# Inverse block products as 32x32 products on the array's diagonal, tied products in the mixers' steps, and x's squares summed on GpSimd, in a one-layer RWKV-7 and gated-delta-rule trunk

## The chip, the cores and the metric

The kernel runs on one core of one Trainium2 chip. The time is the device time of one execution in microseconds (us). Before the change it is 1283.71 us, the median of three runs (1283.25 to 1285.89).

## What is computed

One layer works on x, 256 tokens by 2048 features, all in float32:

```
h = rms_norm(x);  proj = h @ w_in                      # 2048 x 6448
y_a = rwkv7_mixer(proj[:, :3360])                      # 16 heads of 64
y_b = gdn_mixer(proj[:, 3360:])                        # 8 value heads of 128, 4 key heads
x = x + concat(y_a, y_b) @ w_out                       # 2048 x 2048
h = rms_norm(x)
x = x + (silu(h @ w_gate) * (h @ w_up)) @ w_down       # 2048 x 5632, twice, and 5632 x 2048
out = rms_norm(x)
```

Each mixer is a recurrence over time. Both are computed in four chunks of 64 tokens. Inside a chunk the recurrence is a triangular system, so each mixer needs the inverse of a unit triangular 64x64 matrix for each head and chunk, and then passes a state from chunk to chunk. rms_norm needs, for each token, the sum of x's squares over the features.

## The kernel before, in words

**Projections.** Weights come as blocks of 128x1024 (`raw`, three buffers, loaded by SyncE's queue, L168). `halves_of` cuts each block in two halves and splits each half in a high part on ScalarE (`wh`, L177) and a low part on VectorE (`wl`, L178), with four buffers of each. A block of w_in or w_out then gives 24 TensorE products of 256 columns (L199 to L201: high by high, high by low, low by high), of w_gate and w_up 16 (L196, L197), of w_down 24 (L1060). PSUM tag `pb` holds two outputs of projections.

**The mixers run beside the projections.** `prep` (RWKV, per half of the heads), `chain` (RWKV's chunk steps), `gdn_v` and `gdn` are generators, stepped by `tick()` after each group of products. The framework then sets the order of every engine's instructions by a simulated timeline with priorities: what is ready first there stands first. On the chip each engine takes its instructions in that order and waits where an operand is missing.

**Inverses.** `tri_inverse` is called three times: `r` for each RWKV half, `g` for the gated delta rule. It solves 32x32 triangles by a substitution on VectorE (`X`, L325 and L327, 31 steps), writes the result to memory (`sX`, L333) and reads it back in another layout (`st`, L336). The missing off-diagonal 32x32 block of each 64x64 inverse is a product of three 32x32 blocks: first F = B by the one diagonal inverse (`psF`, L351), then F by the other (`psO`, L362). There are 32 such blocks. Four of them are laid on the diagonal of a 128x128 tile that is zero elsewhere (`Bd` and `Fd`, cleared by GpSimd at L338 and L344), so that one product of 128 by 128 by 32 does four blocks: 8 products for `psF`, 8 for `psO`. `Bd` takes the buffer of the substitution's input `A` (tag `i1`), so it is cleared and loaded (`load_bd`, L525 or L837) when the substitution has ended. `tn` (L346, VectorE) is the transposed first half of `st`.

**Steps of the mixers.** RWKV's chunk step has the products R (L545), U (L553), S (L564), Y from the state (L583) and Y from U and V (L585), each as 8 products for 4 pairs of heads and 2 heads, on 64 rows or 64 columns of the array. The delta rule's step has `psK` (L863, full array), `psUg` (L874, 8 products on 64x64), `psSg` (L888, 4 products on 64 rows) and `psOg` (L901, 8 on 64x64). `prep` has `ps_w` and `ps_a` (L403, L404), low-rank products on the upper and the lower 64 rows. A float32 product stands in the trace as two records, one of fp32r as one.

**x's squares.** For the first norm four groups of squares (`sqx`, ScalarE, L274) are halved by VectorE into `ssb` (L275), and 8 float32 products with a constant matrix sum them over partitions (L277), in front of `rstd` (L279, L280).

**The last unit's weights.** The final four feed-forward rows are kept split in SBUF (`wend`, places listed by `wend_slots`), in tiles that the mixers have left.

Of the kernel before, what the change touches and what calls it, by code (L numbers as in the profile page):

```python
# [17 lines left out]
P = 128  # L18
# [31 lines left out]
def trunk_kernel(ctx, tc, xT, vecs, fnw, w_up, a_up, g_up, w_in, w_ab, w_out, w_gu, w_dn, out):  # L50
# [220 lines left out]
    for q in range(4):  # L271
# [39 lines left out]
    def tri_inverse(ip, load_blocks, load_bd, store, dst, nm, psk, sign=1):  # L311
# [3 lines left out]
        load_blocks(A)  # L315
        X = ip.tile([P, 16, 32], F32, tag="i2", name=f"X_{nm}")
# [26 lines left out]
        Fd = ip.tile([P, 8, P], F32, tag="i2", name=f"Fd_{nm}")  # L343
        G.memset(Fd, 0.0)  # L344
# [5 lines left out]
        for g in range(8):  # L350
            PE.matmul(psF3[:, g, :], Bd[:, g, :], tn[:, g, :], start=True, stop=True)  # L351
        for q in range(4):
            qs = slice(q * 32, q * 32 + 32)
            if q % 2:
                S.activation(Fd[qs, :, qs], psF3[qs], AF.Copy, scale=float(sign))
            else:
                V.tensor_scalar(Fd[qs, :, qs], psF3[qs], float(sign), None, ALU.mult)
# [3 lines left out]
        for g in range(8):  # L361
            PE.matmul(psO3[:, g, :], Fd[:, g, :], st[:, 1, g, :], start=True, stop=True)  # L362
# [13 lines left out]
    def prep(hf):  # L376
# [15 lines left out]
        for gr in range(2):  # L392
# [3 lines left out]
            th, sq, al = [], [], []  # L396
            k2 = kt[key]
            sq = rp.tile([P, 2, T], F32, tag="sq2", name=f"sq{hf}{gr}")
            for pi in range(2):
                p = gr * 2 + pi  # L400
                f = hf * 4 + p
                ts = slice(pi * T, pi * T + T)
                PE.matmul(psw[:, ts], lw[0:64, p * P:p * P + P], twa[0:64, :], start=True, stop=True)  # L403
                PE.matmul(psa[:, ts], lw[64:128, p * P:p * P + P], twa[64:128, :], start=True, stop=True)  # L404
                S.activation(sq[:, pi, :], k2[:, pi, :], AF.Square, scale=vc("k_k", f))
            for pi in range(2):
# [97 lines left out]
    def chain(hf):  # L504
# [34 lines left out]
        for ch in range(NCH):  # L539
# [10 lines left out]
            for p in range(4):  # L550
                for h in range(2):
                    hr = slice(h * 64, h * 64 + 64)
                    PE.matmul(U3[hr, p, :], ar[hr, p, ch, 0, :], RR[hr, p, :], start=True, stop=True)  # L553
            for h in range(2):
                hr = slice(h * 64, h * 64 + 64)
                (S.copy, V.tensor_copy)[h](UV[0:64, ch, :, hr], U3[hr])
            yield None
            if ch < NCH - 1:
                psS = mps("psS", "mc")
                S3 = psS[:, 0:256].rearrange("p (a v) -> p a v", a=4)  # L560
                for p in range(4):
                    for h in range(2):
                        hr = slice(h * 64, h * 64 + 64)
                        PE.matmul(S3[hr, p, :], bkn[:, p, ch, hr], UV[:, ch, p, hr], start=True, stop=True)  # L564
# [15 lines left out]
            ph = [(p, h, slice(h * 64, h * 64 + 64)) for p in range(4) for h in range(2)]  # L580
            if ch:
                for p, h, hr in ph:
                    PE.matmul(Y3[hr, p, :], ar[hr, p, ch, 1, :], St[hr, p, :], start=(p == 0), stop=False)  # L583
            for p, h, hr in ph:
                PE.matmul(Y3[hr, p, :], AT[:, h, p, ch, 64:128], UV[:, ch, p, hr], start=(ch == 0 and p == 0),  # L585
                           stop=(p == 3))
# [138 lines left out]
    def gdn():  # L725
# [467 lines left out]
```

## Time and profile before

| | |
|---|---|
| median of the runs | 1283.71 us (1283.25 to 1285.89) |
| the profiled execution's own time | 1289.42 us |
| its span, first to last instruction | 1287.7 us |
| instructions | 23086 |
| TensorE busy (matrix products) | 1264.9 us, 98% |
| weight loads into TensorE | 1127.3 us, 88% |
| VectorE | 930.3 us, 72% |
| ScalarE | 726.7 us, 56% |
| GpSimd | 18.1 us, 1% |
| mean granted TensorE clock | 0.994 of 2.4 GHz |

The projections through w_in and the mixers beside them fill the first 430 us or so, w_out follows to about 540 us, and the feed-forward takes the rest. Busy times of matrix products overlap, since they are pipelined; what a product costs is read from the distance between the starts of neighbours.

### The profile page before, as it was taken

What the parts mean: (1) busy time and instruction counts of PE and PEld (TensorE: products, weight loads), DVE (VectorE), ACT (ScalarE), POOL (GpSimd) and SP (SyncE); (2) the same over time, 40 slices, a digit from 0 to 9 for tenths busy, and PEclk for the clock granted to TensorE, in tenths of its full rate; (3) what the DMA queues carried; (4) which work ended last, traced back from release to release, by engine and by line L of the source; (5) the groups of instructions that cost most, each with busy time, mean ns of one, the idle gap of its engine ahead of it and who ended that gap; (6) DMA issues with size and microseconds to landing.
All of it is one profiled execution on the core that took longest, in us unless ns stands there. A gap on an engine that the chain in (4) does not pass through costs nothing.

```text
span 1287.7 us, 23086 instructions
## 1 busy us (share of the span) xinstructions
PE 1264.9 (98%) x8458; PEld 1127.3 (88%) x8458; DVE 930.3 (72%) x1981; ACT 726.7 (56%) x1469; POOL 18.1 (1%) x66
## 2 busy tenths in 40 slices
PE   8999999999999999999999999999999999999997
PEld 7999999999998899988888888888888888888886
DVE  6988796978864878767766766666767676767664
ACT  7675665666644656666655555545454545555552
POOL 1000000000000000000000000000000000000000
PEclk9999999999999999999999999999999999999999
DMA  7455556464564345556765555555555556565541
GB/s 241 147 167 173 148 171 150 153 183 125 147 211 148 107 141 196 181 171 222 247 195 182 194 184 192 183 194 188 189 188 189 191 186 193 182 196 186 190 148 65
DMA packets 108129, 226.80 MB, mean 176 GB/s; under 512 B 52272, under 2 KB 54448, under 8 KB 107760
## 3 DMA queue, kind: packets, MB, share of 16 engines
q1 hardware_dynamic: 103744, 222.19, 55.2%
q10 hardware_dynamic: 4128, 2.10, 0.6%
q8 instruction: 66, 1.08, 0.3%
q0 software_dynamic: 144, 1.05, 0.2%
q14 instruction: 47, 0.39, 0.1%
HBM read 218.75 MB, written 4.46 MB: 173 GB/s over the span
## 4 chain that ended last, share of the span: by engine, by line
PE 91%; DMA 4%; DVE 2%; ACT 1%; SPq 1%; issue 0%; DVEq 0%; ACTq 0%
PE psb L196 23%; PE psd L1060 17%; PE psb L197 12%; PE psb L201 10%; PE psb L200 9%; PE psb L199 9%; DMA raw_end<-in_w_dn 2%; PE ps_A L464 1%; DVE wl L178 1%; PE psd L1098 1%; PE psd L1096 1%; PE psd L1097 1%; PE psUg L874 1%; DMA raw<-in_w_gu 1%; PE psSg L888 0%; DVE wend L178 0%
## 5 line engine op out<-in xcount | busy, mean ns | idle before, releaser
L177 ACT ACTIVATE wh<-raw 128x512 fp32r<-128x512 f32 x780 | 488.3, 630 | 424.6 <-PE psb L196 137.6
L178 DVE TENSOR_TENSOR wl<-raw,wh 128x512 fp32r<-128x512 f32 x780 | 534.6, 689 | 264.3 <-ACT wh L177 261.1
L196 PE MATMUL psb<-x2s,wh 128*128 128x512 f32 x1408 | 497.4, 398 | 0.0
L197 PE MATMUL psb<-x2s,wl 128*128 128x256 f32 x1408 | 395.2, 282 | 1.5 <-DVE wl L178 1.5
L196 PEld LDWEIGHTS psb<-x2s,wh 128*128 128x128 f32 x1408 | 263.9, 188 | 63.4
L197 PEld LDWEIGHTS psb<-x2s,wl 128*128 128x128 f32 x1408 | 265.9, 189 | 4.9 <-DVE wl L178 2.8
L199 PE MATMUL psb<-xs,wh 128*128 128x256 f32 x816 | 237.1, 291 | 6.3 <-ACT wh L177 6.3
L201 PE MATMUL psb<-xs,wl 128*128 128x256 f32 x816 | 237.1, 292 | 1.7 <-DVE wl L178 1.7
L200 PE MATMUL psb<-xs,wh 128*128 128x256 f32 x816 | 236.9, 291 | 0.0
L1060 PE MATMUL psd<-wh,h 128*128 128x512 f32 x640 | 199.2, 389 | 0.0
L199 PEld LDWEIGHTS psb<-xs,wh 128*128 128x128 f32 x816 | 158.8, 195 | 9.0 <-ACT wh L177 6.3
L201 PEld LDWEIGHTS psb<-xs,wl 128*128 128x128 f32 x816 | 158.6, 195 | 5.0 <-DVE wl L178 3.4
L200 PEld LDWEIGHTS psb<-xs,wh 128*128 128x128 f32 x816 | 158.7, 195 | 3.7 <-issue 2.5
L1060 PEld LDWEIGHTS psd<-wh,h 128*128 128x128 f32 x640 | 119.4, 188 | 24.9
L1060 PE MATMUL psd<-wl,h 128*128 128x512 f32 x320 | 124.4, 389 | 0.0
L200 PE MATMUL psb<-ys,wh 128*128 128x256 f32 x256 | 73.3, 287 | 1.3 <-DVE ys L223 1.3
L199 PE MATMUL psb<-ys,wh 128*128 128x256 f32 x256 | 73.5, 289 | 0.3 <-ACT ys L222 0.3
L201 PE MATMUL psb<-ys,wl 128*128 128x256 f32 x256 | 73.0, 285 | 0.0
L1060 PEld LDWEIGHTS psd<-wl,h 128*128 128x128 f32 x320 | 60.1, 188 | 12.6
L1066 DVE TENSOR_TENSOR acc<-acc,psd 128x512 f32<-128x512 f32 x80 | 51.2, 681 | 2.5 <-PE psd L1060 2.5
L200 PEld LDWEIGHTS psb<-ys,wh 128*128 128x128 f32 x256 | 49.0, 191 | 2.8 <-DVE ys L223 1.7
L199 PEld LDWEIGHTS psb<-ys,wh 128*128 128x128 f32 x256 | 48.8, 191 | 1.8 <-issue 1.2
(316 smaller groups left out, 1088.5 us busy)
## 6 DMA issues: line engine op xcount, KB each, us to landing
raw<-in_w_gu SPq DMA_DIRECT2D x176, 512.0 KB, 3.6
raw<-in_w_in SPq DMA_DIRECT2D x99, 512.0 KB, 3.6
raw<-in_w_dn SPq DMA_DIRECT2D x80, 512.0 KB, 3.5
raw<-in_w_out SPq DMA_DIRECT2D x32, 512.0 KB, 3.5
raw_end<-in_w_dn SPq DMA_DIRECT2D x8, 512.0 KB, 3.9
xraw<-in_xT SPq DMA_DIRECT2D x8, 256.0 KB, 5.8
x<-in_xT SPq DMA_DIRECT2D x1, 2048.0 KB, 11.2
raw<-in_w_ab SPq DMA_DIRECT2D x2, 512.0 KB, 6.0
```

The costliest lines, as they stand in the source:

```text
L177: S.activation(wh, raw[:, hs], AF.Copy)
L178: V.tensor_tensor(wl, raw[:, hs], wh, ALU.subtract)
L196: PE.matmul(ps, wh[:, ks], rt[:, ri, :], start=st, stop=False)
L197: PE.matmul(ps[:, T:], wl[:, ks], rt[:, ri, 0:T], start=False, stop=sp)
L199: PE.matmul(ps[:, 0:T], wh[:, ks], rt[:, ri, 0:T], start=st, stop=False)
L200: PE.matmul(ps[:, 0:T], wh[:, ks], rt[:, ri, T:], start=False, stop=False)
L201: PE.matmul(ps[:, 0:T], wl[:, ks], rt[:, ri, 0:T], start=False, stop=sp)
L464: PE.matmul(psA[h][:, ch, :], bk[hr, ch].rearrange("p a t -> p (a t)"), ar[hr, p, ch].rearrange("p a t -> p (a t)"), start=True, stop=True)
L874: PE.matmul(u3[h % 2 * 64:h % 2 * 64 + 64, h // 2, :], TT[rows, 2 * h + cp, :], vn[rows, cp, h, :], start=True, stop=True)
L1060: PE.matmul(banks[tb * 2 + cg], st, parts[cg][w], start=(i == 0 and w == 0 and st is hh), stop=(i == n - 1 and st is hl))
L1066: V.tensor_tensor(acc[:, tb, cs], acc[:, tb, cs], banks[tb * 2 + cg], ALU.add)
L1096: PE.matmul(ps, hh, wh, start=(i == 0), stop=False)
```

## The change

Four things change.

- **Inverses.** The zero-filled 128x128 tiles go. `Bd` and `Fd` hold 32 columns, get tags of their own (`i5`, `i6`), and `Bd` is loaded at the start of the inverse. `psF` and `psO` become 32 products each of 32 by 32 by 32, at the four diagonal places of the array. One VectorE operation copies `psF` to `Fd` where two of VectorE and two of ScalarE did.
- **Tied products.** `together(ms, after)` makes each product of a list depend, in order alone, on the one ahead of it, and lets the first wait for all operations in `after`. Tied are: the four `ps_w` and `ps_a` products of a group (`low`); the eight of RWKV's U; RWKV's S and both Y products of a chunk, after both copies of U (`my`, `uv`); the four `psK`, after the eight updates of the state (`mk`, `news`); the eight `psUg`, after the eight updates of `vn` (`ready`); and `psSg` with `psOg`, after both copies of `psUg` (`mo`, `ready`).
- **x's squares.** GpSimd adds the four `ssb` groups into one, and 2 products sum it instead of 8.
- **Places.** The tiles of `wend` are listed anew, with one `act` tile in place of `i2` and two fewer of its own.

```diff
+    def together(ms, after=(), sync=True):
+        kind = mybir.DependencyClass
+        for a in after:
+            tc.add_manual_dep(ms[0].ins, a.ins.name, mybir.DependencyInfo(kind.Sync, mybir.DependencyReason.DATA),
+                              reason="together")
+        for a, b in zip(ms, ms[1:]):
+            tc.add_manual_dep(b.ins, a.ins.name, mybir.DependencyInfo(kind.NoSync, mybir.DependencyReason.DATA),
+                              reason="together")
...
         V.tensor_tensor(ssb[:, q], sqx[:, 0:2, :], sqx[:, 2:4, :], ALU.add)
-        for m in range(2):
-            PE.matmul(ps[:, 0:T], half.to_broadcast([P, P]), ssb[:, q, m, :], start=(q == 0 and m == 0),
-                       stop=(q == 3 and m == 1))
+        if q:
+            G.tensor_tensor(ssb[:, 0], ssb[:, 0], ssb[:, q], ALU.add)
+    together([PE.matmul(ps[:, 0:T], half.to_broadcast([P, P]), ssb[:, 0, m, :], start=(m == 0), stop=(m == 1))
+              for m in range(2)])
...
+        Bd = ip.tile([P, 8, 32], F32, tag="i5", name=f"Bd_{nm}")
+        load_bd(Bd)
...
-        Bd = ip.tile([P, 8, P], F32, tag="i1", name=f"Bd_{nm}")
-        G.memset(Bd, 0.0)
-        load_bd(Bd)
...
-        for g in range(8):
-            PE.matmul(psF3[:, g, :], Bd[:, g, :], tn[:, g, :], start=True, stop=True)
...
+        diag = [(g, slice(q * 32, q * 32 + 32)) for g in range(8) for q in range(4)]
+        for g, qs in diag:
+            PE.matmul(psF3[qs, g, :], Bd[qs, g, :], tn[qs, g, :], start=True, stop=True)
+        V.tensor_scalar(Fd, psF3, float(sign), None, ALU.mult)
...
-        for g in range(8):
-            PE.matmul(psO3[:, g, :], Fd[:, g, :], st[:, 1, g, :], start=True, stop=True)
+        for g, qs in diag:
+            PE.matmul(psO3[qs, g, :], Fd[qs, g, :], st[qs, 1, g, :], start=True, stop=True)
...
+            together(low)
...
+            together([PE.matmul(U3[hr, p, :], ar[hr, p, ch, 0, :], RR[hr, p, :], start=True, stop=True)
+                      for p, h, hr in ph])
...
+            together(my, uv)
...
+                together(mk, news)
...
+            together([PE.matmul(u3[h % 2 * 64:h % 2 * 64 + 64, h // 2, :], TT[rows, 2 * h + cp, :],
+                                vn[rows, cp, h, :], start=True, stop=True) for h in range(8)], ready)
...
+            together(mo, ready)
...
-            w = rp.tile([P, 2, 512], F32R, tag="i2", name="wend")
-            yield w[:, 0, :]
-            yield w[:, 1, :]
+            w = act.tile([P, 4, 2 * T], F32R, tag="act", name="wend")
+            for i in range(4):
+                yield w[:, i, :]
```

In the changed program a line of the kernel before has a number 10 to 15 higher: L199 to L201 are L209 to L211 there, L874 is L883, L168 is L178.

**TensorE, the second chunk's `psUg`** (`psUg` is U of the delta rule, `psb` a projection's output). Before:

```order
L874 MATMUL psUg<-vnknSg,TTg 64x128 x2
L199 MATMUL psb<-xs_145,wh 128x256
L874 MATMUL psUg<-vnknSg,TTg 64x128 x2
L200 MATMUL psb<-xs_145,wh 128x256
L201 MATMUL psb<-xs_145,wl 128x256
L874 MATMUL psUg<-vnknSg,TTg 64x128 x2
L199 MATMUL psb<-xs_145,wh 128x256
L874 MATMUL psUg<-vnknSg,TTg 64x128
L200 MATMUL psb<-xs_145,wh 128x256
L874 MATMUL psUg<-vnknSg,TTg 64x128
```

Now:

```order
L210 MATMUL psb<-xs_145,wh 128x256
L211 MATMUL psb<-xs_145,wl 128x256
L883 MATMUL psUg<-vnknSg,TTg 64x128 x8
L209 MATMUL psb<-xs_145,wh 128x256
L210 MATMUL psb<-xs_145,wh 128x256
```

Eight products that stood in five pieces stand in one. Over the whole program `psUg` stands in 15 pieces before and in 5 now.

**SyncE's queue, the inverse `g`** (`X_g` is the substitution's result, `sX_g` and `st_g` its way through memory, `Bd_g` the block B, `TTg` the inverse's place). Before:

```order
L333 DMA sX_g<-X_g 1024x1x32 x2
L837 DMA Bd_g<-sG 32x4x32 x3
L168 DMA raw<-in_w_in 128x1024
L336 DMA st_g<-sX_g 128x8x32 x2
L837 DMA Bd_g<-sG 32x4x32 x2
L168 DMA raw<-in_w_in 128x1024
L837 DMA Bd_g<-sG 32x4x32 x3
L842 DMA TTg<-sX_g 32x16x32 x2
```

Now:

```order
L834 DMA A_g<-sG 16x32x32 x3
L842 DMA Bd_g<-sG 32x4x32 x6
L178 DMA raw<-in_w_in 128x1024
L842 DMA Bd_g<-sG 32x4x32 x2
L178 DMA raw<-in_w_in 128x1024 x5
L610 DMA yl_3613<-in_g_up 128x512
L964 DMA x_6047<-in_xT 128x4096
L611 DMA yl_3613<-in_g_up 32x512
L178 DMA raw<-in_w_in 128x1024 x6
L1029 DMA raw_end<-in_w_dn 128x1024
L346 DMA sX_g<-X_g 1024x1x32 x2
L178 DMA raw<-in_w_in 128x1024
```

The eight loads of `Bd_g` stand ahead of the substitution, next to those of its input `A_g`, instead of behind its result.

**TensorE, the third chunk's S and Y of RWKV's first half.** Before:

```order
L200 MATMUL psb<-xs_244,wh 128x256
L564 MATMUL psS<-UV_485,bkn_484 64x64
L201 MATMUL psb<-xs_244,wl 128x256
```

and nine products of projections further

```order
L200 MATMUL psb<-xs_145,wh 128x256
L564 MATMUL psS<-UV_485,bkn_484 64x64 x7
L583 MATMUL psY<-St_1837,ar_482 64x64 x8
L585 MATMUL psY<-UV_485,AT_483 64x64 x8
L201 MATMUL psb<-xs_145,wl 128x256
```

Now these stand in one piece:

```order
L569 MATMUL psS<-UV_482,bkn_481 64x64 x8
L587 MATMUL psY<-St_1877,ar_479 64x64 x8
L589 MATMUL psY<-UV_482,AT_480 64x64 x8
```

The first product no longer stands alone.

## Rows read from the trace of the kernel before

**Rows 1.** The page's first part, busy time of TensorE (PE) and its weight loads (PEld), share of the span, instructions; and the page's chain of work that ended last, by engine.

```profile
PE 1264.9 (98%) x8458; PEld 1127.3 (88%) x8458; DVE 930.3 (72%) x1981; ACT 726.7 (56%) x1469; POOL 18.1 (1%) x66
...
PE 91%; DMA 4%; DVE 2%; ACT 1%; SPq 1%; issue 0%; DVEq 0%; ACTq 0%
```

**Rows 2.** The list of waits of PE: who waited for whom, us in total, times, longest.

```profile
PE psF_g L351 <- DMA Bd_g<-sG: 2.2, 1, 2.2
PE psb L201 <- DVE wl L178: 1.7, 3, 0.8
...
PE psF_r L351 <- DMA ar<-sX_r: 1.6, 1, 1.6
```

**Rows 3.** Busy time by stretch, for a stretch in the mixers: start:end, length, busy us and instructions of PE, PEld, DVE, ACT, POOL, then the granted clock, the DMA engines' share and GB/s.

```profile
208.00:300.00 92.00, 92.00 (x932) 86.13 (x930) 73.98 (x218) 58.23 (x158) 4.59 (x11) 1.00 0.57 152
```

**Rows 4.** Timeline of PE around the first sum of squares: start us, us, engine, line, operation, records.

```profile
21.32 1.02 PE L277 MATMUL ps_ss<-ssb,vec 128*128 128x256 f32 x4
...
22.30 0.28 PE L200 MATMUL psb<-xs,wh 128*128 128x256 f32 x1
```

**Rows 5.** Timeline of PE around `ps_w` and `ps_a`: one product of each, neighbours, and later two products of `ps_w` alone. One projection product lies in each of the gaps.

```profile
39.44 0.48 PE L403 MATMUL ps_w<-twa,lw 64*128 64x256 f32 x1
...
40.29 0.28 PE L199 MATMUL psb<-xs,wh 128*128 128x256 f32 x1
...
177.81 1.13 PE L403 MATMUL ps_w<-twa,lw 64*128 64x256 f32 x4
...
179.10 0.28 PE L200 MATMUL psb<-xs,wh 128*128 128x256 f32 x1
```

**Rows 6.** Timeline of PE around RWKV's U in one piece, and S in two pieces of 1 and 7 products. One projection product lies in the first gap and one in the second.

```profile
241.77 0.28 PE L201 MATMUL psb<-xs,wl 128*128 128x256 f32 x1
241.98 0.68 PE L553 MATMUL psU<-RR,ar 64*64 64x64 f32 x16
...
242.81 0.28 PE L200 MATMUL psb<-xs,wh 128*128 128x256 f32 x1
...
245.54 0.33 PE L564 MATMUL psS<-UV,bkn 128*64 128x64 f32 x2
...
246.02 0.28 PE L199 MATMUL psb<-xs,wh 128*128 128x256 f32 x1
...
247.06 0.68 PE L564 MATMUL psS<-UV,bkn 128*64 128x64 f32 x14
247.67 0.68 PE L583 MATMUL psY<-St,ar 64*64 64x64 f32 x16
```

**Rows 7.** Timeline of PE around the delta rule's second `psUg` (five pieces, six projection products in the gap), `psSg` and `psOg` (one piece each, one projection product in the gap).

```profile
414.95 0.44 PE L874 MATMUL psUg<-vnknSg,TTg 64*64 64x128 f32 x4
...
418.36 0.28 PE L199 MATMUL psb<-xs,wh 128*128 128x256 f32 x1
...
445.54 1.13 PE L888 MATMUL psSg<-gates,vnknSg 64*128 64x256 f32 x4
...
446.82 0.28 PE L200 MATMUL psb<-ys,wh 128*128 128x256 f32 x1
...
450.92 1.09 PE L901 MATMUL psOg<-vnknSg,gates 64*64 64x128 f32 x16
...
452.16 0.28 PE L200 MATMUL psb<-ys,wh 128*128 128x256 f32 x1
```

**Rows 8.** Timeline of PE around `psF` of the three inverses; in brackets the idle time before and what ended it.

```profile
200.80 0.28 PE L200 MATMUL psb<-xs,wh 128*128 128x256 f32 x1
202.68 2.15 PE L351 MATMUL psF_r<-tn_r,Bd_r 128*128 128x32 f32 x16 [1.60 <-DMA ar<-sX_r]
204.64 0.56 PE L201 MATMUL psb<-xs,wl 128*128 128x256 f32 x1
...
283.87 1.87 PE L351 MATMUL psF_r<-tn_r,Bd_r 128*128 128x32 f32 x16
285.57 0.36 PE L200 MATMUL psb<-xs,wh 128*128 128x256 f32 x1
...
382.47 0.28 PE L200 MATMUL psb<-xs,wh 128*128 128x256 f32 x1
384.97 3.40 PE L351 MATMUL psF_g<-tn_g,Bd_g 128*128 128x32 f32 x16 [2.22 <-DMA Bd_g<-sG]
388.18 0.56 PE L201 MATMUL psb<-xs,wl 128*128 128x256 f32 x1
```

**Rows 9.** Busy time by stretch (columns as in Rows 3) behind the two long waits.

```profile
204.20:207.80 3.60, 3.60 (x19) 3.60 (x19) 2.45 (x6) 1.52 (x3) 0.00 (x0) 0.53 0.57 224
...
388.10:392.10 4.00, 4.00 (x20) 4.00 (x20) 1.53 (x3) 1.38 (x3) 0.00 (x0) 0.51 0.86 264
```

**Rows 10.** Timeline of VectorE and SyncE's queue in the inverse `g`: the substitution's last step, the transposed half `tn_g`, and the last loads of `Bd_g`.

```profile
372.15 0.18 DVE L327 TENSOR_TENSOR X_g<-X_g,tmp_g 128x16 f32<-128x16 f32 x1
...
380.97 0.45 DVE L346 STREAM_TRANSPOSE tn_g<-st_g 128x256 f32<-128x256 f32 x1 [3.31 <-DMA st_g<-sX_g]
...
381.12 1.83 SPq L837 DMA_DIRECT2D Bd_g<-sG  x3
```

**Rows 11.** Groups by line: a GpSimd write of 128x512 and a VectorE sum of the same size (busy us, mean ns | idle before).

```profile
L604 POOL MEMSET yl<- 128x512 f32 x2 | 1.1, 532 | 69.1 <-DVE X_r L327 38.2 <-PE psY L585 31.0
...
L275 DVE TENSOR_TENSOR ssb<-sqx 128x512 f32<-128x512 f32 x4 | 2.8, 692 | 1.4 <-ACT sqx L274 1.4
```

More of the change, by code (lines that the diff above doesn't have):

```diff
@@ L402, in prep @@
                 ts = slice(pi * T, pi * T + T)
-                PE.matmul(psw[:, ts], lw[0:64, p * P:p * P + P], twa[0:64, :], start=True, stop=True)
-                PE.matmul(psa[:, ts], lw[64:128, p * P:p * P + P], twa[64:128, :], start=True, stop=True)
+                low.append(PE.matmul(psw[:, ts], lw[0:64, p * P:p * P + P], twa[0:64, :], start=True, stop=True))
+                low.append(PE.matmul(psa[:, ts], lw[64:128, p * P:p * P + P], twa[64:128, :], start=True, stop=True))
                 S.activation(sq[:, pi, :], k2[:, pi, :], AF.Square, scale=vc("k_k", f))
+            together(low)
             for pi in range(2):
@@ L549, in chain @@
             U3 = psU[:, 0:256].rearrange("p (a f) -> p a f", a=4)
[L550 to L553, printed above, removed]
+            ph = [(p, h, slice(h * 64, h * 64 + 64)) for p in range(4) for h in range(2)]
+            together([PE.matmul(U3[hr, p, :], ar[hr, p, ch, 0, :], RR[hr, p, :], start=True, stop=True)
+                      for p, h, hr in ph])
+            uv = []
             for h in range(2):
                 hr = slice(h * 64, h * 64 + 64)
-                (S.copy, V.tensor_copy)[h](UV[0:64, ch, :, hr], U3[hr])
+                uv.append((S.copy, V.tensor_copy)[h](UV[0:64, ch, :, hr], U3[hr]))
+            my = []
             yield None
@@ L560, in chain @@
                 S3 = psS[:, 0:256].rearrange("p (a v) -> p a v", a=4)
[L561 to L564, printed above, removed]
+                my += [PE.matmul(S3[hr, p, :], bkn[:, p, ch, hr], UV[:, ch, p, hr], start=True, stop=True)
+                       for p, h, hr in ph]
                 Sn = rp.tile([P, 4, C], F32, tag=f"St{ch % 2}", name=f"St{hf}{ch}")
@@ L579, in chain @@
             Y3 = psY[:, 0:256].rearrange("p (a f) -> p a f", a=4)
-            ph = [(p, h, slice(h * 64, h * 64 + 64)) for p in range(4) for h in range(2)]
             if ch:
[L582 to L586, printed above, removed]
+                my += [PE.matmul(Y3[hr, p, :], ar[hr, p, ch, 1, :], St[hr, p, :], start=(p == 0), stop=False)
+                       for p, h, hr in ph]
+            my += [PE.matmul(Y3[hr, p, :], AT[:, h, p, ch, 64:128], UV[:, ch, p, hr], start=(ch == 0 and p == 0),
+                             stop=(p == 3)) for p, h, hr in ph]
+            together(my, uv)
             for h in range(2):
@@ L872, in gdn @@
             u3 = psU.rearrange("p (h f) -> p h f", h=4)
-            for h in range(8):
-                PE.matmul(u3[h % 2 * 64:h % 2 * 64 + 64, h // 2, :], TT[rows, 2 * h + cp, :], vn[rows, cp, h, :],
-                           start=True, stop=True)
+            together([PE.matmul(u3[h % 2 * 64:h % 2 * 64 + 64, h // 2, :], TT[rows, 2 * h + cp, :],
+                                vn[rows, cp, h, :], start=True, stop=True) for h in range(8)], ready)
             if ch < NCH - 1:
@@ L900, in gdn @@
             for h in range(8):
-                PE.matmul(o3[h % 2 * 64:h % 2 * 64 + 64, h // 2, :], gam[rows, h, cp, :], vn[rows, cp, h, :],
-                           start=True, stop=True)
+                mo.append(PE.matmul(o3[h % 2 * 64:h % 2 * 64 + 64, h // 2, :], gam[rows, h, cp, :],
+                                    vn[rows, cp, h, :], start=True, stop=True))
+            together(mo, ready)
             for m in range(2):
```

57 lines of the change are left out of this document (27 added, 30 removed).

## Prediction

> **What bounds the kernel.** I read the shares of busy time first, then the chain of work that ended last [rows 1]: the matrix products are busy for 98% of the span and carry 91% of the chain. The list of TensorE's waits [rows 2] is short, seven rows. Apart from the start of the kernel, only `psF` of two inverses and a few low parts of weights are in it; U, S, Y, `psK`, `psUg` and `psOg` have no row there. In the mixers' stretch TensorE is busy throughout and VectorE for 74 of 92 us [rows 3]. So the time is what TensorE's queue costs, piece by piece, and the measure of a piece is the distance between starts in the timeline, not the busy time, in which pipelined products overlap. One projection product of 256 columns takes 0.12 us from start to start.
>
> A piece of mixer products costs: its start to the first undisturbed projection start behind it, less 0.12 us for each projection product between, plus what the entry costs. U starts 0.21 us behind the projection product ahead of it, not 0.12 [rows 6], so the entry into a piece on part of the array costs 0.09.
>
> **x's squares.** Two products: 22.30 - 21.32 - 0.12 = 0.86 us [rows 4], so 0.43 each. Six of eight go: **2.6 us**. GpSimd's three sums come in place. The trace has none; the nearest rows are a GpSimd write of the size, 0.53 us, and VectorE's sum, 0.69 us [rows 11]; I bound one by 0.53 and twice 0.69, 1.4 us. The two products left stand 12 projection products, 1.4 us, behind the place where the eight ended, which covers the last sum; without cover up to 1.4 us of wait would come back.
>
> **ps_w and ps_a.** One product of each, on different halves of the rows: 40.29 - 39.44 - 0.12 + 0.09 = 0.82 us. Two of `ps_w` alone: 179.10 - 177.81 - 0.12 + 0.09 = 1.26 [rows 5]. By the order, three of the four groups had two such pieces, 2.52, and now have one of four products, twice 0.82 less one entry and exit of 0.19, 1.45. That would be 3.2 us; some pieces stood behind other mixer products and paid less for entry, so I take **3.0 us**.
>
> **RWKV's steps.** U in one piece: 242.81 - 241.98 - 0.12 + 0.09 = 0.80. One product of S alone: 246.02 - 245.54 - 0.12 + 0.09 = 0.45, and the seven left still take 0.61 us to the next step, as eight of U would [rows 6]. So a split costs 0.45. The order has ten before (R 2, U 2, S 4, Y 2) and two now, both in U: **3.6 us**.
>
> **The delta rule's steps.** The second `psUg` costs 418.36 - 414.95 - 6 x 0.12 + 0.09 = 2.78; eight such products in one piece, as `psOg` has them, cost 452.16 - 450.92 - 0.12 + 0.09 = 1.21 [rows 7]. The second and third chunk (five pieces each) save 1.6 each, the fourth (three pieces) some 0.6; the first stays split: 3.8. `psSg` costs 446.82 - 445.54 - 0.12 + 0.09 = 1.25, twice a chunk, and `psOg` 1.21; in one piece two entries and exits go, 2 x 0.19, three times, and the last `psOg` loses a split of 0.5: 1.6. Together **5.4 us**.
>
> **psF and psO.** Undisturbed, eight products take 285.57 - 283.87 = 1.70 us [rows 8]; six such sets. The 32x32 products are not in the trace. Nearest is U, 64 columns on two diagonal tiles: 0.45 for the first product, then (0.80 - 0.45) / 7 = 0.05 each; with 128 columns (`psOg`) eight cost 0.41 more, another 0.05 each. If the price goes with the columns, 0.025, a set of 32 costs 0.40 + 32 x 0.025 = 1.2; if 0.05 is a floor, 0.40 + 31 x 0.05 = 1.95. So six sets give back 3.0 us or lose 1.5. The rows scale with columns down to 64 and stop there; I take 1.5 a set, between: **1.2 us** gained.
>
> **psF's waits.** `psF` of the first inverse starts 202.68 - 200.80 - 0.12 = 1.76 us late and takes 0.26 more than 1.70; behind it, from 204.2 to 207.8, the granted clock is 0.53, the lower of two levels, and 19 products take 3.6 us, some 1.4 too much [rows 8, 9]. For `g`: 384.97 - 382.47 - 0.12 = 2.38 late, 3.21 instead of 1.70, and 20 products in 4.0 us at 0.51, 1.7 too much. Together 3.4 + 5.6 = **9.0 us**. Both waits are for `Bd`: `tn_g` was there at 381.42, while the last `Bd_g` loads were issued from 381.12 [rows 10]. The change loads `Bd` before the substitution. What is late next is `tn`. TensorE came to `psF_g` at 382.47 + 0.12 = 382.59 [rows 8], behind 2273 projection products; by the order it now stands behind 2255, 2.16 us earlier, but four products of 256 columns (the last `ps_g`, 4 x 0.43) that stood ahead of the substitution's end now stand behind it: 382.15. So `tn_g` leads by 0.7 us, if it still comes 9.1 us behind the end of `X_g` at 372.33 [rows 10]. For the first inverse the place is 3 products earlier, for the second there is more room. I keep 1.5 us back for a wait that returns in part: **7.5 us** net.
>
> **At nothing.** GpSimd's clearing of `Bd` and `Fd` goes, off the path. `Fd` becomes one VectorE operation between `psF` and `psO`, which stand at least 22 projection products, 2.6 us, apart. SyncE's queue now has nine small loads between two weight blocks, 9 x 1.83 / 3 = 5.5 us [rows 10], against 24 x 0.12 = 2.9 us for a block; four split halves and three raw blocks, 5.8 us of work and more, cover that, and without them TensorE would wait some 2 us each time. The places of `wend` move loads and splits from one feed-forward unit to later ones, equal in number.
>
> **The sum.** 2.6 + 3.0 + 3.6 + 5.4 + 1.2 + 7.5 = 23.3 us off the profiled execution's 1289.4. The median of the runs is 5.7 us lower, and I take the same off it: 1283.7 - 23.3 = 1260.4, **1260 us**.
>
> **Rivals.**
> - *A start has a floor.* The 32x32 products cost 0.05 us each whatever their columns: six sets lose 1.5 instead of gaining 1.2, and the time is 1263. For it: no piece in the trace has products closer than 0.05. Against: 128 to 64 columns scaled fully. The Trainium skill (TensorE: Matmul & The Clock Gate, Part 1) says that matmul starts come no closer than about 25 ns however few the columns; by that rule two records a product make 0.05, and no run here shows 32-column tiles yet. Chance 0.25.
> - *Waits for `tn`.* `psF` waits for its other operand in place of `Bd`, long enough to lose the clock once or twice; half of 9.0 comes back and what the change says of the inverses is not what happens: 1260 + 3 to 6, near 1265. For: the sequence through memory takes 9.1 us and the lead is 0.7. Chance 0.10.
> - *The feed becomes the bound.* With 14 us less on TensorE in the mixers, VectorE's 80% in [rows 3] rises, and `wl` waits (1.7 us now [rows 2]) eat half of it with some lost clock: 1283.7 - 12 = 1272. Chance 0.13.
> - *Slower: tied pieces wait.* The first product of a tied piece waits for all copies in `after`, and the in-order queue behind it, projections too, stands. One such wait of 1.8 to 2.4 us costs 3.4 to 5.6 with the clock [rows 8, 9]. 18 pieces are tied to copies. From about six such waits on, the gain is gone; with eight the kernel takes 1260 + 8 x 4.5 = 1296. Against: without a tie the last product of each step waited for the same copies, and none shows idle time. Chance 0.06.
> - *No change*, gains and such waits level: 0.04.
>
> **Numbers.** My forecast has 0.42. Faster, by over 0.2% (2.6 us, about what a measurement of this kernel can tell): 0.42 + 0.25 + 0.10 + 0.13 = 0.90; same 0.04; slower 0.06. The low end takes the cheap 32x32 products (1.8 more), the 1.5 held back, and some luck with waits: 1254. The high end is the feed's 1272.
>
> **What would show it.** `ps_ss` with 4 records; `psUg` in five pieces; `psF` with no idle time ahead and no stretch at a clock near 0.5 behind it; a set of 32 products between 1.2 and 1.95 us; the mixers' stretch shorter by some 20 us and the feed-forward unchanged. Idle time in front of a tied piece, or a list of PE's waits that names `wl` or `tn`, would prove me wrong.

## The result, and the profile after

| | median of the runs | lowest to highest | against the kernel before, on the same chip |
|---|---|---|---|
| before | 1284.4 us | 1283.3 to 1285.9 (4 runs) | |
| changed | 1268.0 us | 1265.5 to 1269.2 (4 runs) | ratio 0.9867, 95% interval 0.9851 to 0.9884 |
| changed, a second time | 1264.8 us | 1263.1 to 1267.0 (4 runs) | ratio 0.9842, 95% interval 0.9820 to 0.9864 |

The change takes 16.4 us off in the first comparison and 19.7 us in the second (1284.5 against 1264.8); the forecast was 23.3. The two medians of the changed kernel lie 3.2 us apart, so below some 3 us the experiments tell little. The profiled execution took 1267.8 us, its span 1266.0.

First the page's busy time and the chain of work that ended last, by engine:

```profile
span 1266.0 us, 23603 instructions
PE 1240.0 (98%) x8734; PEld 1109.0 (88%) x8734; DVE 930.5 (73%) x1978; ACT 724.7 (57%) x1463; POOL 17.3 (1%) x63
...
PE 85%; DVE 6%; DMA 5%; ACT 2%; issue 1%; SPq 1%; DVEq 0%; ACTq 0%
```

Against [rows 1], TensorE has more instructions, since a set of 8 products is now one of 32, and is busy for 25 us less; its share stays at 98%, so the kernel is still bound by TensorE's queue, and other engines have gained a little of the chain.

Then where the time went: the span in two stretches, the mixers up to the first product of the feed-forward's gate and up projections, and the rest (columns as in [rows 3]).

```profile
0.00:516.46 516.46, 499.36 (x4820) 476.16 (x4821) 421.32 (x1082) 323.33 (x722) 17.27 (x63) 1.00 0.57 170
516.46:1266.00 749.54, 740.67 (x3917) 632.88 (x3915) 509.14 (x896) 401.39 (x741) 0.00 (x0) 1.00 0.58 186
```

In the trace of before the same product starts at 536.84 us. So 20.4 us of the 21.7 between the two spans lie in the mixers, and the feed-forward is all but unchanged (750.9 and 749.5).

TensorE's waits, columns as in [rows 2]:

```profile
PE psb L211 <- DVE wl L188: 3.4, 8, 1.0
PE psb L210 <- DVE ys L233: 2.2, 1, 2.2
PE psU L558 <- ACT RR L553: 2.0, 2, 1.1
PE psF_g L362 <- DVE tn_g L355: 0.7, 1, 0.7
PE psb L209 <- ACT ys L232: 0.7, 1, 0.7
```

No inverse waits for `Bd` any more; `psF_g` waits 0.7 us for `tn_g`, which is what the prediction named as late next. New is U's wait for the copy `RR`. The waits for `ys`, the input of the second half of `w_out`, are 2.2 + 0.7 us; before they were 0.54 + 0.29 + 0.76.

Next the timeline of TensorE around the changed pieces, to be laid beside [rows 4], [rows 6], [rows 7] and [rows 8]: x's squares, the third chunk's tied `psUg`, the two parts of U that stay split, and `psF_g`.

```profile
31.17 0.28 PE L211 MATMUL psb<-xs,wl 128*128 128x256 f32 x1
31.29 1.02 PE L288 MATMUL ps_ss<-ssb,vec 128*128 128x256 f32 x4
31.96 0.47 PE L209 MATMUL psb<-xs,wh 128*128 128x256 f32 x1
...
207.06 0.29 PE L558 MATMUL psU<-RR,ar 64*64 64x64 f32 x2 [0.84 <-ACT RR L553]
...
208.07 0.68 PE L558 MATMUL psU<-RR,ar 64*64 64x64 f32 x14
208.67 0.38 PE L209 MATMUL psb<-xs,wh 128*128 128x256 f32 x1
...
370.37 0.28 PE L210 MATMUL psb<-xs,wh 128*128 128x256 f32 x1
371.39 0.75 PE L362 MATMUL psF_g<-tn_g,Bd_g 32*32 32x32 f32 x64 [0.75 <-DVE tn_g L355]
372.08 0.39 PE L211 MATMUL psb<-xs,wl 128*128 128x256 f32 x1
372.30 0.28 PE L209 MATMUL psb<-xs,wh 128*128 128x256 f32 x1
...
419.82 1.09 PE L883 MATMUL psUg<-vnknSg,TTg 64*64 64x128 f32 x16
420.84 0.39 PE L210 MATMUL psb<-ys,wh 128*128 128x256 f32 x1
421.07 0.28 PE L211 MATMUL psb<-ys,wl 128*128 128x256 f32 x1
```

The 64 records of `psF_g` take 372.08 - 371.39 = 0.69 us to the next projection product, where eight products of 128x128 took 1.70 [rows 8]; behind them projections start every 0.12 us again, at full clock. By the prediction's measure, from the start to the first undisturbed projection product, such a set costs 372.30 - 371.39 - 0.12 + 0.09 = 0.88, and `psUg` in one piece 421.07 - 419.82 - 0.12 + 0.09 = 1.22, in place of 2.78 with its five pieces [rows 7]; the prediction had 1.21 for it.

Behind `ps_og`, the last mixer product, the changed kernel has its new hole:

```profile
464.12 1.05 PE L934 MATMUL ps_og<-ident,vnknSg 128*128 128x128 f32 x8
465.83 0.50 PE L209 MATMUL psb<-ys,wh 128*128 128x256 f32 x2 [0.66 <-ACT ys L232]
468.49 0.38 PE L210 MATMUL psb<-ys,wh 128*128 128x256 f32 x1 [2.16 <-DVE ys L233]
...
470.29 0.41 PE L211 MATMUL psb<-ys,wl 128*128 128x256 f32 x1
470.50 0.41 PE L209 MATMUL psb<-ys,wh 128*128 128x256 f32 x1
```

TensorE stands for 0.66 + 2.16 us, and from about 469.9 the products start 0.21 us apart for 3.4 us, which costs another 1.5. The granted clock of three of these microseconds, and of three behind them, in the view by stretch, is the lower of the two levels (0.50, 1.2 GHz) and then the higher (1.00, 2.4 GHz):

```profile
470.00:473.00 3.00, 3.00 (x16) 3.00 (x15) 0.69 (x1) 1.12 (x2) 0.69 (x1) 0.50 0.29 120
474.00:477.00 3.00, 3.00 (x27) 3.00 (x26) 2.42 (x5) 2.27 (x5) 0.00 (x0) 1.00 0.77 265
```

To sum this up for all tiles I booked every start-to-start time of TensorE in the mixers on the mixer tile that stands in it or ended just before it, less 0.12 us for a projection product. The table sets the trace of before against that of after; the prediction's terms stand beside it.

| term | booked before, us | booked after, us | saved | forecast |
|---|---|---|---|---|
| x's squares (`ps_ss`) | 3.4 | 0.9 | 2.6 | 2.6 |
| `ps_w`, `ps_a` | 8.9 | 5.7 | 3.2 | 3.0 |
| RWKV: R, U, S, Y | 29.9 | 28.5 | 1.4 | 3.6 |
| delta rule: `psUg`, `psSg`, `psOg` | 22.1 | 15.9 | 6.2 | 5.4 |
| `psF`, `psO`, and the half clock behind `psF` | 17.2 + 2.5 | 5.7 | 14.0 | 1.2 + 7.5 |
| all other tiles and stalls | 61.4 | 68.7 | -7.3 | 0 |
| sum | 145.3 | 125.3 | 20.0 | 23.3 |

### The profile page after: what moved, and what is told of

It is laid out like the page before. It is cut to its first block, busy times and chain, and to the rows that moved or that the text cites. A ratio compares the mean times of both kernels' runs of the same rounds, so it can differ in the third digit from the quotient of the medians.

```text
span 1266.0 us, 23603 instructions
## 1 busy us (share of the span) xinstructions
PE 1240.0 (98%) x8734; PEld 1109.0 (88%) x8734; DVE 930.5 (73%) x1978; ACT 724.7 (57%) x1463; POOL 17.3 (1%) x63
## 4 chain that ended last, share of the span: by engine, by line
PE 85%; DVE 6%; DMA 5%; ACT 2%; issue 1%; SPq 1%; DVEq 0%; ACTq 0%
PE psb L206 24%; PE psd L1070 17%; PE psb L207 12%; PE psb L211 8%; PE psb L210 8%; PE psb L209 8%; DVE wl L188 2%; DMA raw_end<-in_w_dn 1%; DMA raw<-in_w_in 1%; PE ps_A L471 1%; PE psd L1108 1%; PE psd L1106 1%; DMA sA<-AT 1%; PE psd L1107 1%; DMA A_r<-sA 1%
## 5 line engine op out<-in xcount | busy, mean ns | idle before, releaser
L209 PE MATMUL psb<-xs,wh 128*128 128x256 f32 x816 | 234.9, 288 | 6.7 <-ACT wh L187 6.0
L211 PE MATMUL psb<-xs,wl 128*128 128x256 f32 x816 | 235.6, 289 | 3.8 <-DVE wl L188 3.4
L210 PE MATMUL psb<-xs,wh 128*128 128x256 f32 x816 | 233.9, 287 | 0.0
L209 PEld LDWEIGHTS psb<-xs,wh 128*128 128x128 f32 x816 | 157.1, 193 | 9.2 <-ACT wh L187 6.2
L211 PEld LDWEIGHTS psb<-xs,wl 128*128 128x128 f32 x816 | 156.8, 192 | 7.6 <-DVE wl L188 6.8
L210 PEld LDWEIGHTS psb<-xs,wh 128*128 128x128 f32 x816 | 156.9, 192 | 1.7 <-issue 0.5
L209 PE MATMUL psb<-ys,wh 128*128 128x256 f32 x256 | 73.8, 289 | 0.7 <-ACT ys L232 0.7
L211 PE MATMUL psb<-ys,wl 128*128 128x256 f32 x256 | 73.4, 287 | 0.0
L209 PEld LDWEIGHTS psb<-ys,wh 128*128 128x128 f32 x256 | 49.6, 194 | 1.2 <-ACT ys L232 0.9
```

What stands on the lines that cost most here:

```text
L209: PE.matmul(ps[:, 0:T], wh[:, ks], rt[:, ri, 0:T], start=st, stop=False)
L210: PE.matmul(ps[:, 0:T], wh[:, ks], rt[:, ri, T:], start=False, stop=False)
L211: PE.matmul(ps[:, 0:T], wl[:, ks], rt[:, ri, 0:T], start=False, stop=sp)
```

## Experiments

My theory was that three separate savings make the result: pieces that enter part of the array less often, `psF` no longer waiting for `Bd`, and cheaper inverse products. The rivals were that the products' starts have a floor, that ties give back by waits what they save, and that the waits of `psF` belonged to the one profiled execution.

### 1. Each part undone

**No ties.** The helper returns at once:

```
     def together(ms, after=(), sync=True):
+        return
```

> The changed kernel with the helper that ties products made empty: the order of U, S, Y, psK, psUg, psSg, psOg, ps_w and ps_a is again the scheduler's, x's squares and the inverses stay as changed. Theory A (the sum of the prediction): entries and exits of split pieces come back, 3.0 (ps_w, ps_a) + 3.6 (RWKV) + 5.4 (delta rule) = 12 us, so 1268 + 12 = 1280. Theory B (the trace after): ties took 3.2 + 1.4 + 6.2 = 10.8 us out of the pieces, but gave some 4.2 us back (2.0 us of psU waiting for RR is in the 1.4 already; the wait of 2.2 us for ys ahead of w_out's second half, with the clock lost behind it, is not), net 6.6: 1274 to 1275. Rival C: tied pieces wait so often that the ties are worth nothing: 1268, within 2 us.

Measured: 1272.1 us (1271.0 to 1275.4), ratio 0.9912 (0.9897 to 0.9927): 4.1 us above the first median of the changed kernel and 7.3 above the second. Theory B's net 6.6 lies between the two; A's 12 does not, and C's 2 is too small. By the table's booking, the steps' tiles cost 12.0 us more than in the changed kernel, as much as the forecast's 12.0: `psUg` 6.0, `ps_w` and `ps_a` 3.6, S 2.0, Y 1.1, `psOg` 0.8, R 0.7, `psSg` 0.3, less 2.4 for U, which waits here for nothing. TensorE's list of waits has neither `RR` nor `ys`. That the two sums agree is in part chance: without ties this order has `psUg` in 19 pieces, where the kernel before had 15, and U's 2.4 is not a piece's price. From before to after the same tiles save 10.8. So the ties' saving has about the size that was forecast, and they give back some 5 to 8 us of it elsewhere.

**The old inverses** (128x128, zero filling, late `Bd`, and `wend` in its old places):

```
-        Bd = ip.tile([P, 8, 32], F32, tag="i5", name=f"Bd_{nm}")
-        load_bd(Bd)
...
+        Bd = ip.tile([P, 8, P], F32, tag="i1", name=f"Bd_{nm}")
+        G.memset(Bd, 0.0)
+        load_bd(Bd)
...
```

> The changed kernel with the inverses of before (128x128 products on zero-filled Bd and Fd, Bd loaded behind the substitution, wend in its old places); ties and x's squares stay as changed. Theory A: all of the waits of psF and the products' saving go, 7.5 + 1.2 = 8.7 us: 1277. With the after trace's own price of a set (about 0.85 us instead of 1.7, six sets, 5 us) and the waits at their full 9.0: up to 14 us, 1282. Theory B: the profiled execution of before was 5 us longer than any timed one, so most of psF's waits are absent in timed runs; only the products' 5 us and some 1 to 3 us of waits come back: 1274 to 1276, and a profile of it with psF waits under 2 us.

Measured: 1277.4 us (1274.3 to 1278.2), ratio 0.9943 (0.9928 to 0.9959), 9.4 and 12.6 above the two medians. The size fits theory A's 8.7, but not its split; theory B has the sign in the profile (waits of `psF` under 2 us), but its time, 1274 to 1276, is too low. The sets take their old 1.70 us, 6.1 for six (from 0.68); of waits 3 to 6.5 us are left, and not where I had them. In this order `psF` stands with no idle time ahead; other pieces wait instead:

```profile
PE psR L557 <- DVE tmp_g L336: 2.0, 1, 2.0
PE psb L211 <- DVE wl L188: 1.9, 6, 0.8
PE ps_vn L729 <- ACT csv L661: 1.1, 2, 0.8
PE psO_r L373 <- issue: 0.8, 1, 0.8
```

Its trace has three stretches of 3.4 us at a granted clock of 0.50 in the mixers (from 300.9, 335.0 and 478.4 us), the changed kernel's first trace one.

**The squares as before:**

```
-        if q:
-            G.tensor_tensor(ssb[:, 0], ssb[:, 0], ssb[:, q], ALU.add)
-    together([PE.matmul(ps[:, 0:T], half.to_broadcast([P, P]), ssb[:, 0, m, :], start=(m == 0), stop=(m == 1))
-              for m in range(2)])
+        for m in range(2):
+            PE.matmul(ps[:, 0:T], half.to_broadcast([P, P]), ssb[:, q, m, :], start=(q == 0 and m == 0),
+                       stop=(q == 3 and m == 1))
```

> The changed kernel with x's squares as before: eight products, no sums on GpSimd. Theory A: six products of 0.43 us come back, 1268 + 2.6 = 1270.6. Rival: the eight products filled time in which TensorE stands for weights at the start anyway (after has stalls of 0.7, 1.0 and 0.9 us at 18 to 30 us), so that little changes: 1268 to 1269.

Measured: 1270.1 us (1268.7 to 1276.6), 2.1 above the first median, 5.3 above the second; `ps_ss` again books 3.43 us in place of 0.86. Theory A holds in the trace; its size is within what the runs can tell.

### 2. What made `psF` wait

**The load written later, in its own buffer:**

```
         load_blocks(A)
-        Bd = ip.tile([P, 8, 32], F32, tag="i5", name=f"Bd_{nm}")
-        load_bd(Bd)
...
             SY.dma_start(out=st[:, b], in_=sX[b].rearrange("(g q) m j -> (q m) g j", q=4))
+        Bd = ip.tile([P, 8, 32], F32, tag="i5", name=f"Bd_{nm}")
+        load_bd(Bd)
```

> The changed kernel with one thing undone: Bd (32x32 blocks, no zero filling) is loaded behind the substitution, where the kernel before loaded it. This separates the early load from the small products. Theory A (early load is the main part): psF waits for Bd again, 3.4 us idle and some of the 5.6 us of lost clock, so 1268 + 5 to 9 = 1273 to 1277, and psF is in the list of TensorE's waits with 1 us and more. Theory B (the waits came with the zero filling of Bd on GpSimd ahead of the loads, or belong to the one profiled execution): 1268 to 1270.

Measured: 1268.2 us (1267.3 to 1268.6), no difference. But this did not undo the early load. SyncE's row for the last eight loads has the same times as in the changed kernel (first and last issue 313.1 and 320.4 us; there 313.3 and 320.4):

```profile
L842 SPq DMA_DIRECT2D Bd_g<-sG x8: 544/598/1092, 313.1 to 320.4; - x8
```

The scheduler issues a load when its buffer and its data are free, wherever the line stands. So what the change did for the load is the buffer, tag `i5`, that no other tile of the inverse uses.

**`Bd` back in the buffer of the substitution's table**, the load written behind `st`:

```
-        Bd = ip.tile([P, 8, 32], F32, tag="i5", name=f"Bd_{nm}")
+        Bd = ip.tile([P, 8, P], F32, tag="i1", name=f"Bd_{nm}")[:, :, 0:32]
```

> The changed kernel, with Bd back in the buffer of the substitution's table A, so that its loads cannot be issued before the substitution's last step has read A; blocks of 32x32 without zero filling, and the small products, stay. The kernel with the load merely written at the later place took the same time as the changed one (1268.15), and its trace shows the loads issued 60 us before the product all the same. Theory A (the buffer of its own is what took psF's waits away): psF waits for Bd in one or two inverses, 1.5 to 4 us of idle time and lost clock, 1270 to 1274. Theory B (the clearing by GpSimd between the table's last reader and the loads, or the profiled execution, made those waits): psF waits for nothing but tn, 1267 to 1270.

Measured: 1269.7 us (1269.3 to 1275.5), ratio 0.9903 (0.9879 to 0.9926), 1.7 and 4.9 above the two medians. The loads are now issued at 364.0 to 374.8 us, and the waits for `Bd` are back, here in two places of one set, with the half clock behind them:

```profile
373.92 0.25 PE L362 MATMUL psF_g<-tn_g,Bd_g 32*32 32x32 f32 x4 [0.23 <-DVE tn_g L355]
375.37 0.24 PE L362 MATMUL psF_g<-tn_g,Bd_g 32*32 32x32 f32 x2 [1.20 <-DMA Bd_g<-sG]
...
377.98 1.08 PE L362 MATMUL psF_g<-tn_g,Bd_g 32*32 32x32 f32 x58 [1.58 <-DMA Bd_g<-sG]
378.99 0.58 PE L211 MATMUL psb<-xs,wl 128*128 128x256 f32 x1
379.37 0.41 PE L209 MATMUL psb<-xs,wh 128*128 128x256 f32 x1
```

`Bd` isn't cleared by GpSimd in this kernel, so the clearing is not needed for the wait. The median by itself lies in theory B's range, 0.3 under A's; it is the trace that decides for A, with a worth of some 2 to 5 us.

**The kernel before, profiled again**, with no edit:

> The kernel before, unchanged, profiled a second time. The profiled execution that the prediction was made from took 1289.4 us at a mean granted clock of 0.994; the timed runs took 1280.8 to 1286.4 at 0.995 to 0.998. If psF's waits of 1.6 and 2.2 us with their two stretches at half clock belong to that one execution, this profile takes 1281 to 1285 us, and at least one of the two stretches behind psF is absent. If they belong to the kernel, they are both there again, and the time is near 1289.

Measured: 1287.1 us, mean clock 0.995; the 11 timed runs of before beside it took 1279.4 to 1287.9. Both waits are there, but smaller. The clock behind `psF_g` is full; behind `psF_r` it is the lower one for 6.8 us, where the first profile has 3.4:

```profile
202.86 2.39 PE L351 MATMUL psF_r<-tn_r,Bd_r 128*128 128x32 f32 x16 [1.26 <-DMA ar<-sX_r]
205.07 0.56 PE L201 MATMUL psb<-xs,wl 128*128 128x256 f32 x1
205.43 0.41 PE L199 MATMUL psb<-xs,wh 128*128 128x256 f32 x1
...
385.39 1.94 PE L351 MATMUL psF_g<-tn_g,Bd_g 128*128 128x32 f32 x16 [1.49 <-DMA Bd_g<-sG]
387.17 0.37 PE L201 MATMUL psb<-xs,wl 128*128 128x256 f32 x1
387.37 0.28 PE L199 MATMUL psb<-xs,wh 128*128 128x256 f32 x1
```

The row of `psF_r` names a load of `ar`, which isn't an operand of that product. In the first profile that load landed at 202.84 us, behind the start of `psF_r` at 202.68; the last load of `Bd_r`, issued at 197.85, landed at 202.43, and `tn_r` was there at 199.17. So both waits are for `Bd`, as the prediction has it.

So the waits belong to the kernel, and their size to the execution. `psF`, `psO` and the half clock behind `psF` book 14.6 + 1.4 = 16.0 us here and 19.7 in the first profile; the rest after the change is 5.7 and the sets' share of the saving 6.1, which leaves 7.9 for the waits in the first profile and 4.2 in this one; `ps_A`, which here falls into the stretch behind `psF_r`, books 1.0 more on top.

Not every lower clock comes with a wait: this trace has another such stretch among the second chunk's `psUg` pieces, with no idle row of TensorE in the 20 us ahead of it, where the first profile runs at 1.00.

```profile
415.90:419.20 3.30, 3.30 (x18) 3.30 (x17) 3.21 (x5) 2.59 (x4) 0.00 (x0) 0.50 0.02 6
```

It costs 1.5 us. What set it off isn't shown.

### 3. The price of a 32x32 product

In `psF` and in `psO`:

```
-        for g, qs in diag:
+        for g, qs in diag * 4:
```

> The changed kernel with each set of 32 small products, psF and psO, issued four times in a row on the same operands: 18 more sets of 32, to price a product by itself. If a start costs 0.05 us whatever its columns (the floor rival), the 576 added products cost 28.8 us: 1297. If it costs 0.025 us, as one scales U down, 14.4 us: 1282. By the after trace, in which a whole set with entry and exit takes 0.68 us from its first start to the next projection product and four starts lie within some 30 ns, 0.008 us each: 4.6 us, 1272 to 1273.

Measured: 1300.5 us (1297.3 to 1305.6), 32 to 36 us more: all three sizes missed, and the floor's 1297 is near the time by chance. (The smallest took the distance between records for that between products: two records each, 8.5 ns apart, make 9.8 us for 576 products, not 4.6.) Timeline of one of the sets, now of 256 records, `psF` of the first inverse:

```profile
197.29 2.04 PE L362 MATMUL psF_r<-tn_r,Bd_r 32*32 32x32 f32 x218
203.57 0.75 PE L362 MATMUL psF_r<-tn_r,Bd_r 32*32 32x32 f32 x38 [4.24 <-issue]
204.25 1.01 PE L471 MATMUL ps_A<-ar,bk 64*128 64x128 f32 x6
```

The first 218 records start within 199.14 - 197.29 = 1.85 us, 8.5 ns apart; then TensorE stops, with no semaphore that it waits for. Each of the six sets has such a stop, after 159 to 218 records, of 1.6 to 4.4 us, 18.1 us in all. Of the 28.9 us that `psF` and `psO` book more than in the changed kernel, 10.9 are left for the 576 products, 0.019 each. Sets of 64 records have no such stop. Behind the first one, as behind two of the others, the granted clock is 0.50 for 6.8 us, which also slows the pieces that follow:

```profile
203.57:209.70 6.13, 6.13 (x208) 5.62 (x211) 2.87 (x6) 0.59 (x1) 0.00 (x0) 0.50 0.02 6
```

The DMA queues of the two pages point to a cause (queue, kind: packets, MB, share of the 16 engines), the changed kernel first:

```profile
q8 instruction: 69, 1.13, 0.4%
q8 instruction: 78, 1.28, 0.4%
```

Queue q8 moves blocks of 16 KB. Nine more of them come with 2304 more records of products and weight loads on TensorE, 256 to a block, so they look like TensorE's own instructions. At each of the six stops one such block is under way, and TensorE goes on 1.2 to 1.5 us after it has come (in the first, 200.75 to 202.10 us, with the next record at 203.57). So TensorE most likely stood for instructions that had not been loaded; no run varied that loading, so this is argued, not shown.

### 4. The ties' give-back

In the traces the last `psUg` stands behind 10 to 14 projection products more than its pieces did before, since its first product now waits for all eight sums; `ps_og` and `ys` follow it.

**The last chunk's `psUg` no longer tied to its sums:**

```
-                                vn[rows, cp, h, :], start=True, stop=True) for h in range(8)], ready)
+                                vn[rows, cp, h, :], start=True, stop=True) for h in range(8)], ready if ch < NCH - 1 else ())
```

> The changed kernel with one tie loosened: psUg of the last chunk no longer waits for all eight sums before its first product. By the after trace the ties give time back there: psUg of the last chunk stands 10 to 14 projection products later than before, ps_og and the splits of ys follow, and w_out's second half waits 0.7 + 2.2 us for ys and runs 3.4 us at half clock behind it. By the order, the third pair of ps_og now stands ahead of eight fewer products and the split of ys moves ahead of a gate product on VectorE. Theory (that wait is the ties' give-back): the wait of 2.2 us and the stretch at half clock go, 1268 - 3 to 4 = 1264 to 1265, and a split of psUg costs 0.5 to 0.9 of it. Rival (the wait is the tail of the sequence through ScalarE and VectorE, whatever the tie): within 1 us of 1268.

Measured: 1265.9 us (1263.8 to 1268.6), ratio 0.9865 (0.9844 to 0.9887), the changed kernel's own ratio: open. It and three more were then run on one chip.

> The changed kernel, unchanged, beside the three variants below on one chip. Theory: the same as before, 1266 to 1269, with the wait of some 2 us for ys ahead of w_out's second half and a stretch at half clock behind it.

> The kernel of last_free once more, now against the changed kernel on the same chip; alone it took 1265.85, 2.2 us under the changed kernel's 1268.02, but against the runs of before beside it the ratio was the same (0.9865 and 0.9867). Theory (the tie of the last psUg gives back a wait and a stretch of half clock): 2 to 4 us under the changed kernel here. Rival (no gain): within 1 us.

Measured: the changed kernel 1264.8 us (1263.1 to 1267.0), last_free 1266.0 (1264.6 to 1267.1), ratio 0.9850 (0.9829 to 0.9871). My theory of this step falls. The waits for `ys` do shrink from 0.66 + 2.16 us to 0.38 + 0.34 + 0.76, but `psUg` books 1.2 us more, and the half clock behind the wait, on which I had counted, isn't tied to it: the second profile of the changed kernel has the same wait and no such stretch.

```profile
462.10 1.05 PE L934 MATMUL ps_og<-ident,vnknSg 128*128 128x128 f32 x8
463.81 0.50 PE L209 MATMUL psb<-ys,wh 128*128 128x256 f32 x2 [0.66 <-ACT ys L232]
466.47 0.39 PE L210 MATMUL psb<-ys,wh 128*128 128x256 f32 x1 [2.16 <-DVE ys L233]
```

The stretch behind it, by the view of stretches, runs at 1.00:

```profile
468.00:471.00 3.00, 3.00 (x27) 3.00 (x26) 1.41 (x3) 1.42 (x3) 0.69 (x1) 1.00 0.44 180
```

**U of each half's first chunk as one piece**, on top of last_free (`placed` holds the eight copies out of `psO`):

```
-            together([PE.matmul(U3[hr, p, :], ar[hr, p, ch, 0, :], RR[hr, p, :], start=True, stop=True)
-                      for p, h, hr in ph])
+            together([PE.matmul(U3[hr, p, :], ar[hr, p, ch, 0, :], RR[hr, p, :], start=True, stop=True)
+                      for p, h, hr in ph], () if ch else placed)
```

> last_free, and U of the first chunk of each half tied to the copies of the inverse's results, so that it is one piece in place of 1 + 7 products. Theory: two splits of 0.45 us go, and the wait of U for the copy RR (1.7 us in last_free) goes too, since by the order U now stands 30 rows behind R in place of 7: 1 to 2.5 us under last_free. Rival: what U gains, a later piece loses by waiting, since its whole sequence starts some 20 products later: within 1 us of last_free.

Measured: 1267.2 us (1265.8 to 1270.6), ratio 0.9864 (0.9840 to 0.9887), 1.2 above last_free: the rival. The wait for `RR` is gone from the list, but `wl` waits are up from 3.0 us to 5.1, the longest 2.8, and U waits 0.6 for the copies: what U gains, other pieces and the weights' waits take back.

**The last `psUg` as two pieces of four:**

```
+            if ch < NCH - 1:
+                together(mu, ready)
+            else:
+                together(mu[0:4], ready[0:4])
+                together(mu[4:8], ready[4:8])
```

> The changed kernel with psUg of the last chunk tied as two pieces of four, each to its own four sums, in place of one piece of eight tied to all (last_free left it without ties, in 1 + 2 pieces and some single ones). Theory: as last_free, since the second piece stands earlier than or as early as the whole one did and the split of ys again moves ahead of a gate product: 2 to 4 us under the changed kernel. Rival: the wait for ys stays, within 1 us of the changed kernel.

Measured: 1263.7 us (1262.3 to 1265.7), ratio 0.9833 (0.9811 to 0.9854), 1.1 under the changed kernel beside it. The trace does in part as the theory says: `psUg` books only 0.3 us more than tied in one, and the waits for `ys` are 1.1 + 0.3. But 1.1 us is under the theory's 2 to 4 and less than the runs can tell, and their ranges overlap. It is the lowest median of all, not a proven gain.

## Why the prediction was right, and where it was off

- **Direction and range held**; the time, 1268.0 and 1264.8, came out 5 to 8 us above 1260. Of its own signs of being wrong some came, each small: idle time in front of a tied piece (U, 0.84 and 1.1 us), `tn_g` in the list of waits (0.7), and `wl` there (3.4; but it stood there before, with 1.7).
- **x's squares**: 2.6 forecast, 2.6 booked. GpSimd's sum takes 1.61 us, above the bound of 1.4:

```profile
L287 POOL TENSOR_TENSOR ssb<-ssb 128x512 f32<-128x512 f32 x3 | 4.8, 1606 | 19.0 <-DVE ssb L285 19.0
```

  The last ends at 29.39 and `ps_ss` starts at 31.29, so the cover held.
- **Entries and exits of split pieces** (`ps_w`, RWKV, delta rule): 12.0 forecast; 10.8 booked from before to after, 12.0 more in the trace without ties. The price of a piece, read from starts in the timeline and not from busy time, was right: 1.21 forecast for `psUg` in one, 1.22 measured.
- **RWKV's share** was 1.4 in place of 3.6: R, S and Y save 3.5, and U gives 2.1 back, above all by its two waits for `RR`. The prediction had no row for that wait. Its ties' rival priced waits for the copies named in `after`, which U's tie has not, and only at six waits and more. In small, a wait in front of a tied piece did come, and so did the feed's rival, with `wl` waits of 2.4 to 3.4 us in place of 1.5 to 1.7.
- **The inverses' products** were mis-sized the most: 1.2 us forecast, 6.1 by the booking. By the prediction's own measure a set costs 0.88 us, below both its bounds of 1.2 and 1.95 and its 1.5 between them. What failed is, first, the step that went halfway to the floor, and then the price that it scaled from U: 0.40 + 32 x 0.025. Records start 8.9 ns apart, so a product takes 0.018 and the rest of the set 0.31. U uses two tiles of the array and the new products four; that this is the reason isn't shown. The floor rival is refuted for sets of this length: its condition was 0.05 us a product. The Trainium skill (TensorE: Matmul & The Clock Gate, Part 1), cited with it, has about 25 ns as the least distance of starts; here the measurement decides, 8.9 ns.
- **`psF`'s waits**: 7.5 forecast; 7.9 between the first two profiles, 4.2 from the second profile of before (5.2 with `ps_A`), some 3 to 6 in the runs of the old inverses. The mechanism was right, with the buffer and not the place of the load as its cause. The size came from one execution, and the sum then took off its whole 5.7 us offset to the median as if that had nothing to do with the waits. A mean clock of 0.994 among runs at 0.995 to 0.998 says that this execution spent more time at half clock than the median one; some of the 5.7 was most likely in this term already.
- **What was missing**: 7.3 us that other tiles and stalls book more in the first pair of traces. The wait for `ys`, 2.82 us, is 1.2 longer than before's at that place (0.54 + 0.29 + 0.76) and lost 1.5 of clock in one of two profiles; the rest is `wl`, the start, and 0.3 to 0.9 us at several tiles whose order shifted. But in the second pair (before_again and after_again) the same booking has about 143.7 and 120.9 us, 22.8 saved, and the other tiles book only some 1 us more. So most of the 7.3 belongs to the executions and not to the change.

The traces thus save 20.0 and 22.8 us in the mixers, close to the 23.3 of the sum. That closeness is in part luck: the products came out 4.9 us better, against up to 3.3 less for the waits of `psF`, 1.4 to 2.2 less for RWKV's steps, and what the ties give back elsewhere. The medians save less, 16.4 and 19.7. Both profiled executions of before were slower than the median of the runs beside them (1289.4 against 1284.4, 1287.1 against 1283.5), those of the changed kernel were not (1267.8 against 1268.0, 1263.1 against 1264.8).

## What to carry to other kernels

Take a wait's worth from more than one execution before it goes into a sum, and ask whether the profiled one's offset to the median is that wait. A tie of products into one piece saved its entries here as priced, and made the first product as late as the last operand; of the 10.8 to 12 us, 5 to 8 came back elsewhere, and loosening the last one gained nothing that the runs can tell. To load early, give the tile a buffer of its own; where the load stands in the program decided nothing here.

## What the runs showed of the hardware

- 32x32 products on the four diagonal tiles of the array start 8.5 to 8.9 ns apart per record: a set of 64 records takes 0.68 us to the next projection product, against 1.70 for the eight 128x128 products of before.
- A run of 256 such records stops after 159 to 218 of them for 1.6 to 4.4 us, with no semaphore to explain it, and goes on 1.2 to 1.5 us after a 16 KB block of queue q8 (kind: instruction) has come. Here the short instructions were cheap in short sets only.
- The same waits of 0.66 and 2.16 us were followed by 3.4 us at half clock in one execution and by full clock in another; and 3.4 us at half clock came in one profile of before with no idle row in the 20 us ahead.
- A GpSimd sum of 128x512 takes 1.61 us, VectorE's 0.69 [rows 11].
